# A two-layer decoder trunk: Strassen's seven products in the FFN up projection

## The chip, the cores and the metric

One NeuronCore of one Trainium2 chip runs the whole kernel in one launch. The metric is device time in microseconds (us). Besides the timed runs there is one profiled execution, whose trace gives every row below.

## What is computed

The reference is a trunk of two layers on 512 tokens of width 1024, all in float32. Each layer is a hybrid mixer (attention and mLSTM), a cross-attention into 256 memory tokens and a gated MLP with a short causal convolution. Each of the three is preceded and followed by an RMS norm. Only the MLP matters here:

```python
D_MODEL, SEQ, D_FF = 1024, 512, 2816
def conv_ffn(h, w_up, conv_w, conv_b, w_down):
    u = causal_dwconv(h @ w_up, conv_w, conv_b)      # width 3, per column
    a, g = jnp.split(u, 2, axis=-1)
    return (jax.nn.gelu(g, approximate=True) * a) @ w_down
x = x + rmsnorm(conv_ffn(rmsnorm(x, pre_ffn_g), ...), post_ffn_g)
```

`h @ w_up` is 512 x 1024 by 1024 x 5632, in both layers.

## The kernel before

**Precision.** A product of two float32 operands is made of three matmuls in the faster type fp32r. Each operand is split into a high part (a cast on ACT) and a low part (operand minus high part, on DVE), and `mm3` (L108) adds high by high, high by low and low by high in PSUM. The matmuls are all recorded under L102, the transposes under L106.

**Weights.** `load_unit` (L84) brings in one unit of weights: 128 partitions by 1024 floats, 512 KB, by one DMA from the SP queue into a tile `raw`, of which there are two (`PACE["raw"]`). ACT casts it into `whi` (L89), DVE subtracts into `wlo` (L90), each with five buffers. A `raw` buffer is free for the next load when both have read it. For the up projection a unit is one tile of 128 output columns: eight blocks of 128 by 128, one for each 128 rows of K = 1024. Unit 2j holds tile j of the a half and unit 2j + 1 tile j of the g half; the two together are pair j, of 22.

**The up stage** (`ffn`, L944). The norm in front of it leaves the activations with features on partitions, as four tiles `B` (`xn`): high and low part of each half of K, 128 x 4 x 512. Pairs 0 and 1 run through `feat_halves` (L167), first on tokens 0 to 255, then on 256 to 511, while the norm's last tokens still arrive. The other 20 pairs run through `feat_gen` (L156) unit by unit: 8 blocks x 3 matmuls of 512 columns into one PSUM tile `pg`. When a unit is done, `up_done` (L953) makes the convolution: ACT scales and adds the bias (L958), DVE adds the two delayed terms (L960, two instructions). For the g unit ACT applies the gelu (L965) and DVE multiplies by the a tile (L972) into `gt`. `down` (L986) then multiplies the 22 `gt` tiles by `w_down`.

**Order.** PE's order is that of the program text, with other work slipped in by a count of estimated time (`now`, `tick`). The other engines' order is set by a scheduler. Every engine runs its instructions strictly in that order, and so does the SP queue with its loads: one that waits holds up all behind it.

Of the kernel before, what the change touches and what calls it, by code (L numbers as in the profile page):

```python
# [10 lines left out]
F32 = mybir.dt.float32  # L11
# [9 lines left out]
S = 512  # L21
# [17 lines left out]
def trunk_kernel(ctx: ExitStack, tc: tile.TileContext, x4, memt, w, gw, gains, mcw, fcw, gb,  # L39
# [43 lines left out]

    def load_unit(l, i):  # L84
        raw = pp.tile([128, 1024], F32, tag="raw", name=nm("raw"), bufs=PACE["raw"])
        SP.dma_start(raw, w[l, i])
        hi = pp.tile([128, 1024], F32R, tag="whi", name=nm("whi"), bufs=5)
        lo = pp.tile([128, 1024], F32R, tag="wlo", name=nm("wlo"), bufs=5)
        ACT.copy(hi, raw)  # L89
        DVE.tensor_sub(lo, raw, hi.bitcast(F32))  # L90
        return hi, lo

    def split(src, hi, lo):
# [13 lines left out]

    def mm3(o, lh, ll, rh, rl, start, stop):  # L108
        mm(o, lh, rh, start=start, stop=False)
        mm(o, lh, rl, start=False, stop=False)  # L110
        mm(o, ll, rh, start=False, stop=stop)

# [37 lines left out]
    def drain(tasks, filler=iter(())):  # L150
        while alive(tasks):
            if next(filler, filler) is filler:
                now[0] = max(now[0], min(t[1] for t in side))
            tick()

    def feat_gen(l, u, act, done, n=512):  # L156
        hi, lo = load_unit(l, u)
        acc = pg()
        for k in range(8):
            c = slice(128 * k, 128 * k + 128)  # L160
            rh, rl = act(k)
            mm3(acc[:, :n], hi[:, c], lo[:, c], rh, rl, k == 0, k == 7)
            if k == 7:
                done(acc)
            yield

    def feat_halves(l, units, act, dones, between):  # L167
        ws = [load_unit(l, u) for u in units]
        accs = [pg() for _ in units]
        for half in range(2):  # L170
            if half:
                between()
            cc = slice(256 * half, 256 * half + 256)
            for i, (hi, lo) in enumerate(ws):
                for k in range(8):
                    c = slice(128 * k, 128 * k + 128)
                    rh, rl = act(k)
                    mm3(accs[i][:, cc], hi[:, c], lo[:, c], rh[:, cc], rl[:, cc], k == 0, k == 7)
                    if k % 2:
                        yield  # L180
                if half:
                    dones[i](accs[i])
# [41 lines left out]

    HELD = PACE["held"]

    def pre_norm(t, g, xn, wait):
        xt = xs[t]
# [12 lines left out]
        for h in range(2):  # L241
# [3 lines left out]
            xgs.append(xg)  # L245
        yield wait
        for h in range(2):
            to_feature(xgs[h], t, xn[h], xn[2 + h])
            yield PACE["nh"]

    def to_feature(src, t, hi, lo):
# [6 lines left out]
        DVE.tensor_sub(lo[:, :, c], p3, hi[:, :, c].bitcast(F32))  # L258

    def act_of(xn):  # L260
# [4 lines left out]
    class Tail:  # L265
        def __init__(self, l, gpost, gpre, wait, last=False):
            self.wait = wait
            self.es = ExitStack()
            self.gpost = load_gain(l, gpost)
            self.src = None if last else gpre  # L270
            self.xn = None
            self.hg = {}
            self.v = {}
            self.tasks = []

        def open(self):
            if self.src:
                self.gpre = load_gain(*self.src)
                self.xn = [bt(F32R) for _ in range(4)]
            self.tp = self.es.enter_context(tc.tile_pool(name=nm("tail"), bufs=1, reuse_waits="tile"))  # L280

        def consume(self, h, t, acc):
# [9 lines left out]
            hg = self.tp.tile([128, 512], F32, tag="hg", name=nm("hg"), bufs=6)  # L292
            DVE.tensor_mul(hg, acc, self.gpost[:, c])
# [8 lines left out]
            if self.xn is not None:  # L302
                self.tasks.append(spawn(pre_norm(t, (self.gpre[:, :512], self.gpre[:, 512:]), self.xn, self.wait)))

# [638 lines left out]

    def ffn(l, xn, pend):  # L944
        act = act_of(xn)
# [5 lines left out]
        us = {}  # L951

        def up_done(j, half):  # L953
            m = 22 * half + j

            def f(acc):
                u = fp.tile([128, 512], F32, tag=f"u{half}", name=nm("u"), bufs=2)
                ACT.activation(u, acc, AF.Identity, bias=fcw_t[:, m, 3:4], scale=fcw_t[:, m, 2:3])  # L958
                for q in range(1, 3):
                    DVE.scalar_tensor_tensor(u[:, q:], acc[:, :512 - q], fcw_t[:, m, 2 - q:3 - q], u[:, q:],  # L960
                                             ALU.mult, ALU.add)
                us[half] = u
                if half == 0:
                    return
                ACT.activation(u, u, AF.Gelu_apprx_tanh)  # L965
                if j < 16:
                    if j % 4 == 0:
                        us["big"] = bt()
                    gt = us["big"][:, j % 4, :]
                else:  # L970
                    gt = fp.tile([128, 512], F32, tag="gt", name=nm("gt"), bufs=6)
                DVE.tensor_mul(gt, us[0], u)  # L972
                gtiles.append(gt)
            return f

        first = 0
        if pend:
            first = 4
            drain(pend[:2])
            run(feat_halves(l, [U_UP + i for i in range(4)], act, [up_done(i // 2, i % 2) for i in range(4)],  # L980
                            lambda: drain(pend)))
# [4 lines left out]
    def down(l, fp, gtiles, consume):  # L986
        accs = [[pg() for _ in range(4)], [pa() for _ in range(4)]]
# [7 lines left out]
        for k in range(NF):  # L995
            gh_ = fp.tile([128, 512], F32R, tag="gh", name=nm("gh"), bufs=4)
            gl_ = fp.tile([128, 512], F32R, tag="gl", name=nm("gl"), bufs=4)
            split(gtiles[k], gh_, gl_)
# [18 lines left out]
    for l in range(L):  # L1017
# [12 lines left out]
        es, tasks, o_t = cross(l, xn, pend)  # L1030
        tail = Tail(l, G_POST_MEM, (l, G_PRE_FFN), PACE[f"nffn{l}"])

        def cross_done():
            drain(tasks)
            es.close()
            tail.open()

        run(tok_gen(l, U_WO, act_of([o_t[0], o_t[1], o_t[2], o_t[3]]), (0, 1), tail.consume,
                    seq=early(PACE["ec"], cross_done, lambda u: drain(tasks[u:u + 1]))))
        xn = tail.xn  # L1040
        if l == 0:
            run(fill_k(mem_tiles(pool_mem(tail.tp)), 1, range(PACE["kf"][0])))
        pend = tail.tasks
        tail.close()
        es, fp, gtiles = ffn(l, xn, pend)
        last = l == L - 1
        tail = Tail(l, G_POST_FFN, (l + 1, G_PRE_MIX), PACE["nmix"], last)
        tail.open()
        run(down(l, fp, gtiles, tail.consume))
        xn = tail.xn  # L1050
        pend = tail.tasks
        tail.close()
        es.close()


# [76 lines left out]
```

## Time and profile before

| | |
|---|---|
| time, median of 3 runs | 1598.51 us (1597.74 to 1599.52) |
| time of the profiled execution | 1598.33 us |
| its span in the trace | 1596.5 us |
| PE busy | 1576.7 us (99% of the span) |
| DVE, ACT, POOL busy | 949.1 (59%), 778.8 (49%), 64.6 us (4%) |
| granted TensorE clock | 0.999 of full |

The span is what the trace covers from first to last instruction; the time of the run has 1.8 us around it. A busy share says how long an engine had an instruction in it, not that it was at its peak: matmuls are pipelined, so what one costs is read from the distance between the starts of two, not from its own length. In a row of the timeline, "x2" merges two instructions, and brackets give the idle time before and who ended it.

### The profile page before, as it was taken

To read this page: it belongs to the slowest core of one execution; us is meant where nothing else is said; L and a number is where in the kernel's file an instruction comes from. 1 tells how busy PE (TensorE), PEld (TensorE's weight loads), DVE (VectorE), ACT (ScalarE), POOL (GpSimd) and SP (SyncE) were. 2 spreads that over 40 slices of the span, in tenths; PEclk is the share of its full clock that TensorE was granted. 3 is DMA by queue.
4 is the path that set the end of the run, shared out by engine and by line. 5 is a ranking of instruction groups with operands and counts; after the bars stand their busy time and mean duration, and the time that the engine had idled before them with its cause. 6 is when DMAs were issued, how large, how long until landed. Compare 5 with 4: busy or idle time off the path is not lost.

```text
span 1596.5 us, 21066 instructions
## 1 busy us (share of the span) xinstructions
PE 1576.7 (99%) x8032; PEld 1328.4 (83%) x8032; DVE 949.1 (59%) x1664; ACT 778.8 (49%) x1354; POOL 64.6 (4%) x92
## 2 busy tenths in 40 slices
PE   7999999999999999999999999999999999999998
PEld 5788888998898888888887888889888888888886
DVE  5688555746666555543376876557557655555334
ACT  5677574544554333332356775745445433333222
POOL 0000210100000000000010001101001000000000
PEclk9999999999999999999999999999999999999999
DMA  5322244551253222322323222444512332232221
GB/s 177 124 94 73 95 142 147 160 183 67 67 187 97 102 92 97 101 93 95 103 86 112 93 72 87 144 143 156 171 41 82 106 98 100 93 99 99 93 97 62
DMA packets 55414, 172.91 MB, mean 108 GB/s; under 512 B 6801, under 2 KB 9617, under 8 KB 55314
## 3 DMA queue, kind: packets, MB, share of 16 engines
q1 hardware_dynamic: 55314, 171.57, 32.7%
q8 instruction: 63, 1.03, 0.3%
q14 instruction: 37, 0.30, 0.1%
HBM read 165.22 MB, written 6.33 MB: 107 GB/s over the span
## 4 chain that ended last, share of the span: by engine, by line
PE 87%; DMA 5%; DVE 4%; ACT 3%; issue 1%; POOL 1%; SPq 0%; POOLq 0%; DVEq 0%; ACTq 0%
PE pg L102 69%; PE pa L102 14%; PE pa L106 3%; DMA raw<-in_w_dram 3%; DVE wlo L90 1%; ACT whi L89 1%; DMA raw<-in_memt_dram 1%; DMA raw<-dv 1%; DVE xg L244 1%; DMA raw<-dk 1%; POOL sm L217 0%; ACT junk L222 0%; DVE x L299 0%; DMA dk<-kf 0%; POOL sq L630 0%
## 5 line engine op out<-in xcount | busy, mean ns | idle before, releaser
L102 PE MATMUL pg<-B,whi 128*128 128x512 f32 (+1 forms) x2432 | 693.4, 371 | 2.2 <-DVE ql L925 2.2
L90 DVE TENSOR_TENSOR wlo<-raw,whi 128x1024 fp32r<-128x1024 f32 x268 | 328.8, 1228 | 283.1 <-ACT whi L89 282.7
L102 PEld LDWEIGHTS pg<-B,whi 128*128 128x128 f32 x2432 | 431.6, 189 | 70.0 <-DVE ql L925 2.6
L102 PE MATMUL pg<-B,wlo 128*128 128x512 f32 (+1 forms) x1216 | 447.1, 368 | 0.0
L89 ACT CAST whi<-raw 128x1024 fp32r<-128x1024 f32 x268 | 281.3, 1050 | 293.6 <-PE pg L102 224.7
L102 PE MATMUL pg<-whi,B 128*128 128x512 f32 x896 | 297.5, 398 | 0.0
L102 PEld LDWEIGHTS pg<-B,wlo 128*128 128x128 f32 x1216 | 229.2, 189 | 38.6
L102 PEld LDWEIGHTS pg<-whi,B 128*128 128x128 f32 x896 | 168.5, 188 | 35.1 <-DVE B L95 1.3
L102 PE MATMUL pg<-wlo,B 128*128 128x512 f32 x448 | 175.2, 391 | 0.6 <-DVE sm L236 0.6
L960 DVE SCALAR_TENSOR_TENSOR u<-pg,fcw,u 128x511 f32<-128x511 f32 (+1 forms) x176 | 131.4, 747 | 3.1
L102 PEld LDWEIGHTS pg<-wlo,B 128*128 128x128 f32 x448 | 84.7, 189 | 15.9 <-DVE wlo L90 1.0
L217 POOL TENSOR_TENSOR sm<-sm,mhalf 128x1 f32<-128x1 f32 x56 | 34.3, 612 | 1183.7 <-DVE sm L290 1007.4
L965 ACT ACTIVATE u<-u 128x512 f32<-128x512 f32 x44 | 27.8, 633 | 85.3 <-DVE u L960 85.3
L102 PE MATMUL pa<-whi,gh 128*128 128x512 f32 x176 | 68.6, 390 | 0.0
L102 PE MATMUL pg<-whi,gh 128*128 128x512 f32 x176 | 68.6, 390 | 0.0
L102 PE MATMUL pa<-whi,gl 128*128 128x512 f32 x176 | 68.5, 389 | 0.0
L102 PE MATMUL pa<-wlo,gh 128*128 128x512 f32 x176 | 68.5, 389 | 0.0
L102 PE MATMUL pg<-whi,gl 128*128 128x512 f32 x176 | 68.5, 389 | 0.0
L102 PE MATMUL pg<-wlo,gh 128*128 128x512 f32 x176 | 68.5, 389 | 0.0
L958 ACT ACTIVATE u<-pg,fcw 128x512 f32<-128x512 f32 x88 | 68.1, 774 | 0.0
L95 DVE TENSOR_TENSOR gl<-B,gh 128x512 fp32r<-128x512 f32 x32 | 22.1, 692 | 76.5 <-ACT gh L94 76.4
L94 ACT CAST gh<-B 128x512 fp32r<-128x512 f32 x32 | 19.9, 623 | 92.1 <-PE pg L102 87.0
(215 smaller groups left out, 1956.4 us busy)
## 6 DMA issues: line engine op xcount, KB each, us to landing
raw<-in_w_dram SPq DMA_DIRECT2D x268, 512.0 KB, 3.3
gain<-in_gains_dram SPq DMA_DIRECT2D x11, 512.0 KB, 3.7
raw<-in_memt_dram SPq DMA_DIRECT2D x20, 256.0 KB, 3.0
tb<-tb_d SPq DMA_DIRECT2D x16, 256.0 KB, 4.0
x<-in_x_dram SPq DMA_DIRECT2D x8, 256.0 KB, 5.4
e<-nmu_d SPq DMA_DIRECT2D x8, 256.0 KB, 3.7
dv<-vf SPq DMA_DIRECT2D x8, 256.0 KB, 2.8
dk<-kf SPq DMA_DIRECT2D x16, 128.0 KB, 3.5
```

The lines of the kernel that those rows point to most:

```text
L89: ACT.copy(hi, raw)
L90: DVE.tensor_sub(lo, raw, hi.bitcast(F32))
L94: ACT.copy(hi, src)
L95: DVE.tensor_sub(lo, src, hi.bitcast(F32))
L102: PE.matmul(o, lhs, rhs, **kw)
L106: PE.transpose(o, src, idn)
L217: POOL.tensor_tensor(r, v, mhalf[:, :1], ALU.pow)
L244: DVE.scalar_tensor_tensor(xg, xt[:, c], r, g[h], ALU.mult, ALU.mult)
L958: ACT.activation(u, acc, AF.Identity, bias=fcw_t[:, m, 3:4], scale=fcw_t[:, m, 2:3])
L960: DVE.scalar_tensor_tensor(u[:, q:], acc[:, :512 - q], fcw_t[:, m, 2 - q:3 - q], u[:, q:], ALU.mult, ALU.add)
L965: ACT.activation(u, u, AF.Gelu_apprx_tanh)
```

## The change

Pairs 2 to 21 of each layer are computed by the Strassen-Winograd form. The 2 x 2 blocks are: of the activations, K half by token half (A); of the weights, K half by column tile (B; b11 and b21 are the halves of the a unit, b12 and b22 those of the g unit). Eight products of quarters become seven, each of 4 blocks of K x 3 matmuls of 256 columns: 84 matmuls of 256 columns for a pair in place of 48 of 512.

- **Sums of weights** (`weights`, L1063): POOL makes four sums of 128 x 512 for each pair (L1067 to L1070) into two tiles `T` of 128 x 1024, called t12 and t34 here. ACT and DVE then split four things: the a unit (128 x 1024), t12, t34, and b22 (128 x 512, tile `b`, one buffer). The first three use `whi` and `wlo`, which still have five buffers; `raw` still has two.
- **Sums of activations** (`Forms.add`, L296): `pre_norm` also leaves the activations in float32 (ACT, L275), and when the third and fourth token tiles arrive DVE makes four sums of 128 x 512 for each and splits two of 128 x 1024.
- **Products** (`up_products`, L1053): PE's order for pair j is product 5, 6, then 4 of pair j - 1, 1 of pair j + 1, then 2, 3, 7. The sums of products are made partly by accumulating in PSUM and partly by three copies of 128 x 256 on ACT (L1103, L1121, L1131) and two additions of 128 x 256 on DVE (L1123, L1132). Four matmuls of 512 columns per layer only set PSUM's state.
- **Elsewhere**: the product of gelu and a goes from DVE to POOL (L1041); some of `gt`, the `gh`/`gl` of `down` and the tail's `hg` move into the tiles of `Forms`; `whi` and `wlo` are 1152 wide and used at an offset of 32 floats in the halves and products.

```diff
-    def load_unit(l, i):
+    def load_raw(l, i):
         raw = pp.tile([128, 1024], F32, tag="raw", name=nm("raw"), bufs=PACE["raw"])
         SP.dma_start(raw, w[l, i])
...
+    def w_split(raw, off=0):
+        hi = pp.tile([128, 1152], F32R, tag="whi", name=nm("whi"), bufs=5)[:, off:off + 1024]
+        lo = pp.tile([128, 1152], F32R, tag="wlo", name=nm("wlo"), bufs=5)[:, off:off + 1024]
+        split(raw, hi, lo)
         return hi, lo
...
+        def add(self, t, xf):
+            self.xf[t] = xf
+            if t < 2:
+                return
...
+            DVE.tensor_add(a22, a21, a22)
+            DVE.tensor_sub(a21, a11, a21)
+            DVE.tensor_sub(a11, a22, a11)
+            DVE.tensor_sub(a12, a12, a11)
...
+                split(f, self.s[i][:, :, c], self.s[i + 1][:, :, c])
...
-                DVE.tensor_mul(gt, us[0], u)
+            POOL.tensor_tensor(gt, us.pop((j, 0)), us.pop((j, 1)), ALU.mult)
...
-        for i in range(first, 2 * NF):
-            run(feat_gen(l, U_UP + i, act, up_done(i // 2, i % 2)))
+        run(up_products(l, xn, forms, range(2, NF), up_conv))
...
+        def weights(j):
+            ra, rg = load_raw(l, U_UP + 2 * j), load_raw(l, U_UP + 2 * j + 1)
+            b11, b21, b12, b22 = ra[:, :512], ra[:, 512:], rg[:, :512], rg[:, 512:]
+            t12, t34 = forms.flat(), forms.flat()
+            POOL.tensor_tensor(t12[:, :512], b12, b11, ALU.subtract)
+            POOL.tensor_tensor(t12[:, 512:], b22, t12[:, :512], ALU.subtract)
+            POOL.tensor_tensor(t34[:, :512], b22, b12, ALU.subtract)
+            POOL.tensor_tensor(t34[:, 512:], b21, t12[:, 512:], ALU.subtract)
+            wa = w_split(ra, HALF_OFF)
+            wt = w_split(t12, HALF_OFF)
+            wb = forms.pool.tile([128, 1120], F32R, tag="b", name=nm("b"))
+            wb = wb[:, 96:608], wb[:, 608:1120]
+            split(b22, *wb)
+            wu = w_split(t34, HALF_OFF)
+            return {1: (wa, 0), 2: (wa, 512), 5: (wt, 0), 6: (wt, 512), 3: (wb, 0), 7: (wu, 0), 4: (wu, 512)}
...
+            yield from product(e5, w_, 5, True)
+            p5 = forms.pool.tile([128, 256], F32, tag="p5", name=nm("p5"), bufs=2)
+            ACT.copy(p5, e5)
+            yield from product(e1, w_, 6)
+            DVE.tensor_add(G[:, hv[0]], e1, p5)
+            if j > pairs[0]:
+                yield from last(j - 1)
+            if j < pairs[-1]:
+                yield from first(j + 1)
+            yield from product(A[:, hv[0]], w_, 2)
+            yield from product(G[:, hv[0]], w_, 3)
+            yield from product(e1, w_, 7)
+            ACT.copy(A[:, hv[1]], e1)
+            DVE.tensor_add(G[:, hv[1]], e1, p5)
+            done(j, 1, G)
```

How the built program's order changes is shown at two places. The first is DVE in the middle of the up stage of layer 0. Before, one pair looks like this (`wlo` is a unit's low part, `u` the convolution, the last row the product of gelu and a):

```order
L90 TENSOR_TENSOR wlo_5801<-raw_5798,whi_5800 128x1024
L960 SCALAR_TENSOR_TENSOR u_5649<-pg_5624,fcw_4646,u_5649 128x511
L960 SCALAR_TENSOR_TENSOR u_5649<-pg_5624,fcw_4646,u_5649 128x510
L90 TENSOR_TENSOR wlo_5838<-raw_5835,whi_5837 128x1024
L960 SCALAR_TENSOR_TENSOR u_5684<-pg_5659,fcw_4646,u_5684 128x511
L960 SCALAR_TENSOR_TENSOR u_5684<-pg_5659,fcw_4646,u_5684 128x510
L972 TENSOR_TENSOR B_5689<-u_5649,u_5684 128x512
```

With the change, from t34 of one pair (T_6494; its units are raw_6489 and raw_6491) to b22 of the next (t12 and t34 are T_6620 and T_6621, the units raw_6616 and raw_6618), DVE has:

```order
L100 TENSOR_TENSOR wlo_6511<-T_6494,whi_6510 128x1024
L100 TENSOR_TENSOR wlo_6627<-raw_6616,whi_6626 128x1024
L100 TENSOR_TENSOR b_6507<-raw_6491,b_6507 128x512
L1132 TENSOR_TENSOR pg_4933<-pa_6432,p_1252_6527 128x256
L1024 SCALAR_TENSOR_TENSOR u_6611<-pg_4933,fcw_4652,u_6611 128x511
L1123 TENSOR_TENSOR pg_4935<-pa_6559,p_1268_6654 128x256
L1024 SCALAR_TENSOR_TENSOR u_6611<-pg_4933,fcw_4652,u_6611 128x510
L1024 SCALAR_TENSOR_TENSOR u_6681<-pg_4932,fcw_4652,u_6681 128x511
L1024 SCALAR_TENSOR_TENSOR u_6681<-pg_4932,fcw_4652,u_6681 128x510
L100 TENSOR_TENSOR wlo_6631<-T_6620,whi_6630 128x1024
L100 TENSOR_TENSOR wlo_6638<-T_6621,whi_6637 128x1024
L100 TENSOR_TENSOR b_6634<-raw_6618,b_6634 128x512
```

The split of b22 (the last reader of the g unit's `raw`) stands behind the low parts of t12 and t34 in both pairs; in the first pair it also stands behind the low part of the next pair's a unit (raw_6616), in the second it does not. ACT's casts stand in the same two orders, and the two alternate over the stage.

The second place is POOL. Before, it has nothing in the up stage: its rows pass from the norms before the stage to those after it (each row is one reciprocal root of a norm).

```order
L217 TENSOR_TENSOR sm_4386<-sm_4384,mhalf 128x1
L217 TENSOR_TENSOR sm_4432<-sm_4430,mhalf 128x1
L217 TENSOR_TENSOR sm_4446<-sm_4444,mhalf 128x1
L217 TENSOR_TENSOR sm_7050<-sm_7048,mhalf 128x1
L217 TENSOR_TENSOR sm_7064<-sm_7062,mhalf 128x1
```

With the change it has five instructions for each pair, here from one product of gelu and a to the next:

```order
L1041 TENSOR_TENSOR B_5921<-u_6299,u_6229 128x512
L1067 TENSOR_TENSOR T_6365<-raw_6363,raw_6361 128x512
L1069 TENSOR_TENSOR T_6366<-raw_6363 128x512
L1068 TENSOR_TENSOR T_6365<-raw_6363,T_6365 128x512
L1070 TENSOR_TENSOR T_6366<-raw_6361,T_6365 128x512
L1041 TENSOR_TENSOR B_6430<-u_6426,u_6356 128x512
```

The first of the four sums reads both units (raw_6361 is a, raw_6363 is g), and the fourth is the last of them that reads the a unit.

## Rows read from the trace of the kernel before

**Rows 1.** Windows: start and end of norm, then up stage; engines' busy us, clock, DMA.
```profile
444.00:469.00 25.00, 25.00 (x214) 25.00 (x213) 12.59 (x17) 10.63 (x18) 1.40 (x1) 1.00 0.63 205
480.00:640.00 160.00, 160.00 (x708) 132.48 (x707) 90.27 (x107) 61.19 (x77) 0.00 (x0) 1.00 0.30 99
```
**Rows 2.** Timeline of PE in the up stage: start, length, matmuls of 512 columns.
```profile
565.78 0.61 PE L102 MATMUL pg<-B,whi 128*128 128x512 f32 x2
...
566.46 0.61 PE L102 MATMUL pg<-B,whi 128*128 128x512 f32 x2
```
**Rows 3.** Timeline of PE in the halves of pairs 0 and 1: matmuls of 256 columns.
```profile
474.87 0.40 PE L102 MATMUL pg<-B,whi 128*128 128x256 f32 x2
...
475.23 0.40 PE L102 MATMUL pg<-B,whi 128*128 128x256 f32 x2
```
**Rows 4.** Groups of DVE by line and shape: count, busy us, mean ns of one, idle before.
```profile
L90 DVE TENSOR_TENSOR wlo<-raw,whi 128x1024 fp32r<-128x1024 f32 x268 | 328.8, 1228 | 283.1 <-ACT whi L89 282.7
L960 DVE SCALAR_TENSOR_TENSOR u<-pg,fcw,u 128x510 f32<-128x510 f32 x88 | 65.9, 749 | 3.1
...
L972 DVE TENSOR_TENSOR B<-u,u 128x512 f32<-128x512 f32 x32 | 22.1, 692 | 21.3 <-ACT u L965 21.3
L95 DVE TENSOR_TENSOR gl<-B,gh 128x512 fp32r<-128x512 f32 x32 | 22.1, 692 | 76.5 <-ACT gh L94 76.4
...
L95 DVE TENSOR_TENSOR B<-pg,B 128x256 fp32r<-128x256 f32 x16 | 6.7, 421 | 12.0 <-ACT B L94 12.0
```
**Rows 5.** Groups of ACT by line and shape, the same columns.
```profile
L89 ACT CAST whi<-raw 128x1024 fp32r<-128x1024 f32 x268 | 281.3, 1050 | 293.6 <-PE pg L102 224.7 <-DMA raw<-in_w_dram 61.3 <-issue 3.2
L958 ACT ACTIVATE u<-pg,fcw 128x512 f32<-128x512 f32 x88 | 68.1, 774 | 0.0
...
L965 ACT ACTIVATE u<-u 128x512 f32<-128x512 f32 x44 | 27.8, 633 | 85.3 <-DVE u L960 85.3
...
L94 ACT CAST gh<-B 128x512 fp32r<-128x512 f32 x32 | 19.9, 623 | 92.1 <-PE pg L102 87.0 <-DVE B L972 5.1
...
L94 ACT CAST B<-pg 128x256 fp32r<-128x256 f32 x16 | 6.0, 373 | 19.2 <-PE pg L102 15.4 <-DVE B L95 3.6
```
**Rows 6.** POOL's instructions of L630 and L747: ns min/median/max, first and last start.
```profile
L630 POOL TENSOR_TENSOR sq<-sq,sq x6: 1292/1295/2237, 120.2 to 969.0; 128x512 f32<-128x512 f32 x6
...
L747 POOL TENSOR_TENSOR e<-e,mask x8: 1283/1417/2631, 182.3 to 1030.2; 128x512 f32<-128x512 f32 x8
```
**Rows 7.** Timeline of POOL and DVE around 170 us and around 232 us.
```profile
169.70 2.23 POOL L630 TENSOR_TENSOR sq<-sq,sq 128x512 f32<-128x512 f32 x1 [27.00 <-ACT sq L629]
...
169.58 1.22 DVE L90 TENSOR_TENSOR wlo<-raw,whi 128x1024 fp32r<-128x1024 f32 x1
...
231.42 1.28 POOL L747 TENSOR_TENSOR e<-e,mask 128x512 f32<-128x512 f32 x1 [5.37 <-ACT whi L89]
...
231.72 2.06 DVE L90 TENSOR_TENSOR wlo<-raw,whi 128x1024 fp32r<-128x1024 f32 x1
```
**Rows 8.** Loads of `raw`: landing in the up stage; then DVE, SP, ACT near 322 us.
```profile
DMA to landing us min/median/max: 3.2/3.3/3.4
...
320.77 1.23 DVE L90 TENSOR_TENSOR wlo<-raw,whi 128x1024 fp32r<-128x1024 f32 x1 [1.90 <-ACT whi L89]
...
322.02 0.33 SPq L86 DMA_DIRECT2D raw<-in_w_dram  x1
...
325.80 1.05 ACT L89 CAST whi<-raw 128x1024 fp32r<-128x1024 f32 x1 [1.46 <-DMA raw<-in_w_dram]
```
**Rows 9.** Waits of the SP queue: line, waited for, us in total, times, longest.
```profile
SPq L86 <- DVE wlo L90: 932.8, 201, 12.3
```
**Rows 10.** Timeline of PE at the kernel's start.
```profile
11.54 1.97 PE L106 MATMUL pa<-ident,xg 128*128 128x128 f32 x8 [5.42 <-DVE xg L244]
...
14.52 1.05 PE L102 MATMUL pg<-whi,B 128*128 128x512 f32 x2
15.37 0.46 PE L102 MATMUL pg<-wlo,B 128*128 128x512 f32 x1
```

More of the change, by code (lines that the diff above doesn't have):

```diff
@@ L82, in load_gain, with load_unit @@
         return g
-    def load_unit(l, i):
+    def load_raw(l, i):
         raw = pp.tile([128, 1024], F32, tag="raw", name=nm("raw"), bufs=PACE["raw"])
         SP.dma_start(raw, w[l, i])
[L87 to L90, printed above, removed]
+        return raw
+    def w_split(raw, off=0):
+        hi = pp.tile([128, 1152], F32R, tag="whi", name=nm("whi"), bufs=5)[:, off:off + 1024]
+        lo = pp.tile([128, 1152], F32R, tag="wlo", name=nm("wlo"), bufs=5)[:, off:off + 1024]
+        split(raw, hi, lo)
         return hi, lo
+    def load_unit(l, i, off=0):
+        return w_split(load_raw(l, i), off)
     def split(src, hi, lo):
@@ L154, in drain @@
             tick()
+    HELD = PACE["held"]
+    HALF_OFF = 32
+    PAD_S = 6
     def feat_gen(l, u, act, done, n=512):
@@ L223, in sumsq, with pre_norm @@
         return s_
-    HELD = PACE["held"]
-    def pre_norm(t, g, xn, wait):
+    def pre_norm(t, g, xn, wait, forms=None):
         xt = xs[t]
@@ L246, in pre_norm, with to_feature @@
         yield wait
+        while forms and t == 3 and not forms.s:
+            yield 0.2
+        xf = forms.piece() if forms else None
         for h in range(2):
-            to_feature(xgs[h], t, xn[h], xn[2 + h])
+            to_feature(xgs[h], t, xn[h], xn[2 + h], xf[:, 4 * h:4 * h + 4, :] if forms else None)
             yield PACE["nh"]
-    def to_feature(src, t, hi, lo):
+        if forms:
+            while not forms.free:
+                yield 0.2
+            forms.add(t, xf)
+    def to_feature(src, t, hi, lo, f32=None):
         p = pa()
@@ L265, in trunk_kernel, with __init__ @@
     class Tail:
-        def __init__(self, l, gpost, gpre, wait, last=False):
+        def __init__(self, l, gpost, gpre, wait, last=False, forms=None, room=None):
             self.wait = wait
+            self.forms = forms
+            self.room = room
             self.es = ExitStack()
@@ L951, in ffn @@
         us = {}
-        def up_done(j, half):
[L954 to L971, printed above, removed]
-                DVE.tensor_mul(gt, us[0], u)
-                gtiles.append(gt)
-            return f
@@ L976, in ffn, with up_conv @@
[L976 to L981, printed above, removed]
-        for i in range(first, 2 * NF):
-            run(feat_gen(l, U_UP + i, act, up_done(i // 2, i % 2)))
-        return es, fp, gtiles
-    def down(l, fp, gtiles, consume):
+        def up_conv(j, half, acc):
+            m = 22 * half + j
+            u = fp.tile([128, 512], F32, tag=f"u{half}", name=nm("u"), bufs=2)
+            ACT.activation(u, acc, AF.Identity, bias=fcw_t[:, m, 3:4], scale=fcw_t[:, m, 2:3])
+            for q in range(1, 3):
+                DVE.scalar_tensor_tensor(u[:, q:], acc[:, :512 - q], fcw_t[:, m, 2 - q:3 - q], u[:, q:],
+                                         ALU.mult, ALU.add)
+            if half:
+                ACT.activation(u, u, AF.Gelu_apprx_tanh)
+            us[j, half] = u
+            if (j, 1 - half) not in us:
+                return
+            if j < 16:
+                if j % 4 == 0:
+                    us["big"] = bt()
+                gt = us["big"][:, j % 4, :]
+            elif j < 18:
+                if j == 16:
+                    us["gain"] = pp.tile([128, D], F32, tag="gain", name=nm("gt"), bufs=2)
+                gt = us["gain"][:, 512 * (j - 16):512 * (j - 16) + 512]
+            else:
+                gt = fp.tile([128, 512], F32, tag="gt", name=nm("gt"), bufs=4)
+            POOL.tensor_tensor(gt, us.pop((j, 0)), us.pop((j, 1)), ALU.mult)
+            gtiles.append(gt)
@@ L987, in down @@
+    def down(l, forms, gtiles, consume):
         accs = [[pg() for _ in range(4)], [pa() for _ in range(4)]]
@@ L1041, in trunk_kernel @@
         if l == 0:
-            run(fill_k(mem_tiles(pool_mem(tail.tp)), 1, range(PACE["kf"][0])))
+            run(fill_k(mem_tiles(lambda: tail.forms.wide(F32R)), 1, range(PACE["kf"][0])))
+            tail.forms.free = True
         pend = tail.tasks
         tail.close()
-        es, fp, gtiles = ffn(l, xn, pend)
+        forms = tail.forms
+        es, fp, gtiles = ffn(l, xn, pend, forms)
         last = l == L - 1
-        tail = Tail(l, G_POST_FFN, (l + 1, G_PRE_MIX), PACE["nmix"], last)
+        tail = Tail(l, G_POST_FFN, (l + 1, G_PRE_MIX), PACE["nmix"], last, room=forms.flat)
         tail.open()
-        run(down(l, fp, gtiles, tail.consume))
+        run(down(l, forms, gtiles, tail.consume))
         xn = tail.xn
```

105 lines of the change are left out of this document (93 added, 12 removed).

## Prediction

> **What bounds the kernel now.** I first read the windows of the up stage [rows 1]: in 160 us PE is busy for 160, DVE for 90, ACT for 61 and POOL for none. No engine but PE is near its limit, so a stage costs what its matmuls cost. That cost is the distance between starts. Three matmuls of 512 columns take 566.46 - 565.78 = 0.68 us, 0.227 each [rows 2]; three of 256 take 475.23 - 474.87 = 0.36 us, 0.120 each [rows 3]. A pair now costs 48 x 0.227 = 10.88 us, 20 pairs 217.6 us, twice. Next to be read is how a load of weights is released: the SP queue spends 933 us waiting for a DVE low part, 201 times [rows 9], because there are two `raw` buffers. Today this wait is idle time without a price: a unit's work on ACT and DVE is 1.05 + 1.23 us [rows 4, 5] and a load 3.3 us [rows 8], against 10.88 / 2 = 5.44 us of PE for a unit, with two buffers.
>
> **PE's part.** A pair becomes 84 x 0.120 = 10.08 us, 0.80 less. If nothing else counted, 40 pairs would save 32 us. The four extra matmuls per layer cost 0.9 us.
>
> **The other engines' part, per pair.** DVE: three low parts of 1.228, one of 0.692 (b22), four convolution terms of 0.749, two additions of 0.421 (nearest row, a 128 x 256 subtraction from PSUM) [rows 4]: 8.2 us, before 6.1. ACT: three casts of 1.050, one of 0.623, two of 0.774, a gelu of 0.633, three copies of 0.373 [rows 5]: 7.1 us. POOL: five instructions of 128 x 512 with two inputs; the trace has such ones at 1.29 us when alone [rows 6], so 6.5 us. Each of these fits under 10.08. What decides is in which order they wait for each other.
>
> **POOL and DVE block each other.** At 169.70 a POOL instruction that takes 1.29 us alone took 2.23: DVE had begun a low part at 169.58, which ended at 170.80, and POOL ended 1.13 us after that. At 231.72 DVE began a low part while POOL ran until 232.70; it took 2.06 us and ended 1.08 after POOL [rows 7]. So a POOL sum and a DVE subtraction with both inputs in SBUF run one after the other, the second in 1.13 or 1.08 us from the first's end.
>
> **The loop of releases.** The a unit's `raw` is free when POOL's fourth sum has read it; the g unit's when DVE has made the low part of b22. POOL's first sum needs the g unit. In DVE's and ACT's fixed order b22 stands behind t12 and t34, which come out of POOL's sums of the same pair, and in every second pair also behind the next pair's a unit. So the g load of the next pair cannot start before POOL has finished this pair, and POOL cannot start the next pair before that load has landed. From one g load's issue to the next:
>
> - A pair whose b22 follows t34 directly: load 3.3 [rows 8]; four sums 4 x 1.29 = 5.16 [rows 6]; then low part of t12, blocked until the fourth sum ends, 1.08; POOL's product of gelu and a, which is ready and waits its turn, 1.13; low part of t34, 1.08 [rows 7]; low part of b22, 0.69 [rows 4]. Sum 12.4.
> - A pair whose b22 also follows the next a unit: load 3.3; four sums 5.16; only now is the a unit's buffer free, so the a load, 3.3; its cast 1.05, its low part 1.23, then b22 0.69. Sum 14.7.
>
> Each has some eight hand-overs of 0.02 to 0.03 us (the load at 322.02 was issued 0.02 after the low part that ended at 322.00 [rows 8]): 0.25. Together 27.6 for two pairs, **13.8 us a pair** against 10.88. PE then has 3.7 us of idle time in each pair, and its 0.80 is worth nothing.
>
> How often: pairs 2 to 21 are 20, and the loop holds in the 18 steps from the second's weights to the last's; the first pair's weights are made during the halves and the last has none to make. 18 x (13.8 - 10.88) = 52.6; the other two pairs save 1.6; at the end of the stage the first `gh` and `gl` of the down projection must wait for tiles that product 7 of the last pair reads, and cost a cast and a subtraction in sight, 0.62 + 0.69 [rows 4, 5], before partly hidden; the first wait of the loop in a layer adds about as much. That makes 53 a layer, **106 for both**.
>
> **What lies beside other work.** The float32 copies, activation sums and splits come in the stretch of the norm and the halves: for two token tiles DVE has 2 x (4 x 0.69 + 2 x 1.23) = 10.4 us and ACT some 9, where 25 us have 12.6 and 10.6 busy [rows 1]. They fit in the remaining 12 to 14; without that cover they delay product 5 of the first pair by up to 3 us a layer. I take 0. The copies into PSUM, the additions and the convolution lie between the terms of the loop. The gelu product leaves DVE (0.69) for POOL, where it stands in the loop in every second pair (above). The new places of `gt` and `hg` change no count of instructions. The offset of 32 floats could change the 0.120: in the halves 0.1175 would be 2 us in all; inside the loop nothing.
>
> **Bounds.** The load: 3.2, to the 3.78 us from issue to ACT's start near 322 us [rows 8]. The sum on POOL: 1.13 if one follows another as it followed DVE [rows 7], to 1.42, the median with company [rows 6]. The gelu product: nothing if it is late, to 1.13. All low: 3.2 + 4.52 + 1.08 + 1.08 + 0.69 = 10.6 and 3.2 + 4.52 + 3.2 + 2.97 = 13.9, 12.2 a pair, +47 us. All high: 3.78 + 5.68 + 3.98 + 0.25 = 13.7 and 3.78 + 5.68 + 3.78 + 2.97 + 0.25 = 16.5, 15.1 a pair, +151 us. I take the middle values since they come from this very stage or from undisturbed rows.
>
> A price by page: the Trainium skill, GPSIMD Engine Reference (Elementwise, side-by-side cycle accounting), gives 4497 ns for such an addition of 2048 elements, so by estimate 1.12 us for 512; the trace's 1.29 differs, and by the page the loop would be 0.7 us a pair shorter and the kernel 24 us faster than I say.
>
> **The sum.** The profiled execution took 1598.33 us, as good as the median of 1598.51. 1598.3 + 106 = 1704, and 1705 is the forecast.
>
> **Rivals.**
> - *PE stays the bound (faster).* For it: no engine has more than 8.2 us of work in a pair. Then 1598 - 32 + 2 + about 3 for the stage's ends = 1571. It decides where the loop of releases comes to 20.16 us in two pairs; all but the POOL sums is 27.6 - 10.3 = 17.3, so eight sums would have to take 0.36 us each, against 1.29. It could only come about if the g unit's buffer were free earlier than I read from the order. Chance 0.05.
> - *The shared access is the bound (no change).* If the loop were loose but POOL and DVE excluded each other, a pair would cost 5 x 1.29 + 3 x 1.23 + 0.69 = 10.8 us, 10.88 before: 1598, at most 1600. It needs the same freedom. Chance 0.03.
> - *PE's clock falls in the new gaps (slower still).* After 5.4 us of idle at the start, matmuls of 512 columns stood 0.43 us apart (14.52 to 15.37) instead of 0.227 [rows 10]: the level of 1.2 instead of 2.4 GHz. A pair at the lower level takes 84 x 0.12 x 0.43 / 0.227 = 19 us, and if it held all through, 40 x (19 - 10.9) = +325, 1923. Against it: the gaps are 1 to 3 us each and several in a pair, the work between them is 10 us, and there is slack: product 3, for which the next cast of b22 waits, ends six products (8.6 us) and 1 to 3 us of waiting for copies after t12's low part, and that cast comes 15 us after it by the terms above (14.7 - 9.5 + 8.5 + 1.05). A slower PE for part of the time then costs nothing. A mild form, 15 to 16 us a pair, gives 1750 to 1790. Chance 0.07. The Trainium skill, TensorE: Matmul & The Clock Gate (Part 1), says that the throttled state is the default and that activity releases it, by which idle PE is a risk of its own; these rows agree in the level.
>
> **How the numbers follow.** The forecast has 0.85. Its bounds, 1645 to 1749, with little of the clock's mild form, make the range 1650 to 1755. Differences within 0.2% (3.2 us) can hardly be told from no change in this kernel. Faster 0.05 and the same 0.03 are the first two rivals, slower the rest, 0.92.
>
> **What would show it.** In the changed profile PE busy falls well under 90% in the up stage; the starts of POOL's first sum stand alternately near 12.7 and 15 us apart; a g load is issued right behind each low part of b22, and POOL's first sum starts when it lands; POOL has instructions of up to 2.3 us. The 256-column matmuls stand 0.12 apart. I am wrong if POOL's first sum waits for something else, if PE is busy all through the stage, or if matmuls in it stand 0.22 apart.

## The result, and the profile after

The changed kernel takes 1726.67 us (median of 4 runs, 1721.86 to 1729.15) against 1598.12 us on the same chip: 1.080 times as long, 95% interval 1.0773 to 1.0828. The forecast was 1705 us (1650 to 1755), slower. The profiled execution took 1721.86 us; its span is 1720.1 us, 123.6 us more than before.

Part 1 of the page of the changed kernel, busy us and share of the span:

```profile
PE 1597.7 (93%) x9480; PEld 1404.3 (82%) x9480; DVE 1083.9 (63%) x1804; ACT 895.1 (52%) x1578; POOL 368.5 (21%) x296
```

The up stages hold nearly all of the difference. From pair 2 to the start of the down projection they lasted 217.6 us in either layer; now 274.9 and 280.7. Windows of the two stages, columns as in [rows 1]:

```profile
476.00:751.00 275.00, 225.81 (x1687) 216.67 (x1686) 179.44 (x203) 135.05 (x204) 142.38 (x97) 0.94 0.24 80
1312.00:1593.00 281.00, 229.61 (x1685) 220.30 (x1686) 179.44 (x204) 137.47 (x207) 142.50 (x98) 0.93 0.25 83
```

No engine is full: PE is busy for 82%, DVE for 65, POOL for 52. Before, PE was never idle in the window of [rows 1]. The waits of PE in the first window say for whom it now waits (us in total, times, longest): for casts of sum tiles, for their low parts, and for a copy (L1131) that stands on ACT behind the casts of the next a unit and, in every second pair, of b22.

```profile
PE pa L107 <- ACT whi L99: 18.9, 10, 2.6
PE pg L107 <- ACT pg L1131: 15.5, 12, 1.7
PE pa L107 <- DVE wlo L100: 11.9, 15, 0.9
```

What they wait for in turn is in the chain of waits, here for two pairs (start, length, engine and line; hand-overs and two middle sums left out):

```profile
578.39 1.28 POOL T L1067
...
582.26 1.29 POOL T L1070
...
583.57 3.45 DMA raw<-in_w_dram
...
587.10 1.05 ACT whi L99
...
589.33 0.68 DVE b L100
...
590.04 3.63 DMA raw<-in_w_dram
...
593.80 1.29 POOL T L1067
...
597.63 1.28 POOL T L1070
...
598.93 1.05 ACT whi L99
...
602.15 0.69 DVE b L100
...
602.86 3.47 DMA raw<-in_w_dram
...
606.46 1.29 POOL T L1067
```

This is the forecast's loop of releases, and TensorE is not in it; from 598.66 to 602.23 DVE makes the two low parts, 1.32 and 2.22 us long. The second, which the chain waits for, is the one that is held up, by POOL's product of gelu and a, which runs until 601.14. From first sum to first sum the pair that starts at 578.39 takes 15.41 us: sums, a second load (the next a unit), its cast, b22, the g load. The pair at 593.80 takes 12.66: sums, cast, low parts, b22, the g load. In layer 0 there are 18 such steps: the first 17.60, then nine with a mean of 12.73 and eight with 15.36; their mean is 14.17, layer 1's 14.23 (1316.69 to 1572.78).

SP's waits in the first window say the same from the side of the loads: where all 41 waited for low parts before, now 19 wait for the fourth sum and 20 for the low part of b22 (L1132 is the addition that follows it); 12 more, 24.0 us in all, are for another low part.

```profile
SPq L86 <- POOL T L1070: 141.7, 19, 8.8
SPq L86 <- DVE pg L1132: 53.0, 9, 6.6
SPq L86 <- DVE b L100: 42.2, 11, 7.5
SPq L86 <- DVE wlo L100: 24.0, 12, 5.2
```

Which kind a pair is, the compiled order on DVE decides. From the list of DVE's instructions, two pairs of layer 0 (low parts of sum tiles T, of the next a unit, of b22):

```
641 wlo<-T   642 wlo<-T   643 wlo<-raw (next a)   644 b<-raw
651 wlo<-T   652 wlo<-T   653 b<-raw   654 wlo<-raw (next a)
```

The text of the kernel is the same for every pair; the scheduler chose the order, and turns it round from pair to pair.

### The profile page after: what moved, and what is told of

Its sections match the earlier page's. It is cut to its first block, busy times and chain, and to the rows that moved or that the text cites. A ratio compares the mean times of both kernels' runs of the same rounds, so it can differ in the third digit from the quotient of the medians.

```text
span 1720.1 us, 24569 instructions
## 1 busy us (share of the span) xinstructions
PE 1597.7 (93%) x9480; PEld 1404.3 (82%) x9480; DVE 1083.9 (63%) x1804; ACT 895.1 (52%) x1578; POOL 368.5 (21%) x296
## 4 chain that ended last, share of the span: by engine, by line
PE 49%; DMA 16%; POOL 13%; DVE 9%; issue 7%; ACT 6%; POOLq 0%; SPq 0%; DVEq 0%; ACTq 0%
PE pg L107 33%; DMA raw<-in_w_dram 14%; PE pa L107 13%; ACT whi L99 3%; POOL T L1069 3%; POOL T L1070 3%; POOL T L1067 3%; POOL T L1068 3%; PE pa L111 2%; DVE wlo L100 2%; DVE b L100 1%; DMA raw<-in_memt_dram 1%; POOL sm L226 1%; ACT junk L231 1%; DVE xg L252 1%
## 5 line engine op out<-in xcount | busy, mean ns | idle before, releaser
L107 PE MATMUL pg<-B,whi 128*128 128x256 f32 (+1 forms) x1800 | 425.2, 329 | 36.9 <-ACT pg L1131 30.9
L107 PEld LDWEIGHTS pg<-B,whi 128*128 128x128 f32 x1800 | 293.3, 191 | 61.0 <-ACT pg L1131 35.6
L107 PE MATMUL pg<-B,wlo 128*128 128x256 f32 (+1 forms) x896 | 288.7, 322 | 0.0
L107 PE MATMUL pa<-S,whi 128*128 128x256 f32 x960 | 203.1, 310 | 43.6 <-ACT whi L99 39.5
L100 DVE TENSOR_TENSOR wlo<-T,whi 128x1024 fp32r<-128x1024 f32 x80 | 137.6, 1720 | 122.4 <-ACT whi L99 121.0
L107 PEld LDWEIGHTS pa<-S,whi 128*128 128x128 f32 x960 | 168.4, 215 | 48.8 <-ACT whi L99 44.0
L107 PE MATMUL pa<-S,wlo 128*128 128x256 f32 x480 | 152.1, 317 | 24.3 <-DVE wlo L100 24.2
L1024 DVE SCALAR_TENSOR_TENSOR u<-pg,fcw,u 128x510 f32<-128x510 f32 (+1 forms) x176 | 128.1, 745 | 33.7 <-ACT u L1022 31.2
L107 PE MATMUL pa<-whi,S 128*128 128x512 f32 x352 | 117.5, 393 | 0.0
L107 PE MATMUL pg<-whi,S 128*128 128x512 f32 x352 | 116.1, 390 | 0.8 <-DVE u L1024 0.8
L1067 POOL TENSOR_TENSOR T<-raw,raw 128x512 f32<-128x512 f32 x40 | 53.0, 1325 | 276.7 <-DMA raw<-in_w_dram 188.9
```

The lines of the kernel that those rows point to most:

```text
L100: DVE.tensor_sub(lo, src, hi.bitcast(F32))
L107: PE.matmul(o, lhs, rhs, **kw)
L1067: POOL.tensor_tensor(t12[:, :512], b12, b11, ALU.subtract)
```

## The experiments

Each run was timed beside the kernel before, on the same chip as it (medians of the kernel before: 1596.6 to 1597.3 us).

| run | edit | median us | ratio to before, 95% interval |
|---|---|---|---|
| e1_raw4 | four raw buffers | 1624.85 | 1.0186 [1.0163, 1.0208] |
| e2_b22_first | b22 split early, its tile with two buffers | 1635.54 | 1.0241 [1.0223, 1.0259] |
| e3_double_product5 | product 5 twice | 1789.41 | 1.121 [1.1193, 1.1227] |
| e4_gelu_product_dve | gelu product on DVE | 1672.78 | 1.0477 [1.0462, 1.0493] |
| e5_b22_before_next | order fixed: b22 first | 1682.08 | 1.0527 [1.0512, 1.0541] |
| e6_b22_after_next | order fixed: b22 last | 1844.43 | 1.1554 [1.1533, 1.1575] |
| e7_b22_after_double5 | as e6, product 5 twice | 1840.65 | 1.1523 [1.1507, 1.1539] |
| e8_every_second_pair | seven products in every second pair | 1601.41 | 1.0023 [1.0013, 1.0032] |
| e9_plain_unshifted | as e8, plain pairs at column 0 | 1602.56 | 1.0043 [1.003, 1.0056] |
| e10_three_of_four | in three pairs of four, one order fixed | 1589.77 | 0.9954 [0.9941, 0.9967] |
| e11_no_weight_sums | weight sums left out | 1569.63 | 0.983 [0.9814, 0.9847] |
| e12_raw4_t12_order | as e1, with e10's order | 1632.22 | 1.0211 [1.0194, 1.0228] |

### Opening the loop: e1 and e2

```diff
-            ra, rg = load_raw(l, U_UP + 2 * j), load_raw(l, U_UP + 2 * j + 1)
+            ra = load_raw(l, U_UP + 2 * j)
+            rg = fp.tile([128, 1024], F32, tag="rg", name=nm("rg"), bufs=2)
+            SP.dma_start(rg, w[l, U_UP + 2 * j + 1])
```

> Only in the stage of the seven products, the second raw unit of a pair gets a pair of buffers of its own (four raw buffers there instead of two; the room comes from letting the last four gelu products use buffers that are idle by then). Nothing is computed otherwise. Theory 1, the loop of releases through the raw buffers (load 3.5 us, sums 5.1 us, ACT and DVE work on them, 12.7 and 15.3 us in turn): the next pair's loads no longer wait for this pair's low parts, so the waits of POOL for a load (188.9 us) nearly vanish and the time falls by 80 to 125 us, to 1600 to 1645 us, where the next limit is TensorE's own 10.1 us or the 10.8 us of POOL and DVE together. Theory 2, TensorE at half clock is what costs the time: loads come earlier but the stretches at half clock stay, and the time falls by less than 25 us. Theory 3, POOL's and DVE's blocking of each other is the limit: no change, within 10 us, since the same instructions block each other.

```diff
+            wb = forms.pool.tile([128, 1120], F32R, tag="b", name=nm("b"), bufs=2)
+            wb = wb[:, 96:608], wb[:, 608:1120]
+            split(b22, *wb)
             wt = w_split(t12, HALF_OFF)
-            wb = forms.pool.tile([128, 1120], F32R, tag="b", name=nm("b"))
-            wb = wb[:, 96:608], wb[:, 608:1120]
-            split(b22, *wb)
```

> Two raw buffers as in the changed kernel. The split of quarter b22 is written ahead of the split of the first sum tile instead of behind it, and its tile has two buffers so that it need not wait for product 3 of the pair before. Theory 1, the loop: the second unit's buffer is now released by the last sum that reads it, and both loads of the next pair leave when the four sums are done; the loop becomes 3.7 us of load and hand-over and 5.1 us of sums, 8.9 us, less than TensorE's 10.1, so the time falls by 80 to 120 us, to 1605 to 1645 us. Theory 2, the half clock: under 25 us less. Theory 3, the blocking of POOL and DVE: within 10 us, as no instruction is added or removed.

102 and 91 us less than the changed kernel: both inside theory 1's ranges, far from the 25 and 10 us of the others. More buffers, or an earlier release of the same two, free the same time; so the time lay in the release. (In e2, too, the last four gelu products use buffers that are idle by then.) But e2's steps did not fall to the 8.9 us that I expected: one goes from 562.15 to 573.47, 11.3 us, with 6.4 for the four sums, of which the first is blocked (2.20 us), and 4.3 for the g load, which is issued behind the a load. What still stands above the kernel before, e12 looks at below.

### TensorE's work, and an order that moved with it: e3, e6, e7

```diff
             yield from product(e5, w_, 5, True)
+            yield from product(e5, w_, 5, True)
```

> Product 5 of every pair is computed twice into the same bank, the second run writing over the first: 12 more matmuls a pair, 1.44 us, 57.6 us over both layers, and nothing else. Theory 1, the loop of releases does not pass through TensorE, which waits 49 us in a layer's stage: the time stays within 20 us of the changed kernel's 1727, most of the added work filling waits. Theory 2, the half clock costs the time: the added work fills the pauses behind which the clock falls, so that less of the stage runs at half clock and the time falls by 10 to 40 us. If TensorE's own work is on the path after all: 45 to 60 us longer, 1770 to 1787 us.

It took 63 us more, near the 57.6 of work added: by the numbers, TensorE on the path. The trace says otherwise. The chain by line in e3, 580 to 650 us, holds no PE row:

```profile
by line: DMA raw<-in_w_dram 45.4%; issue 12.9%; POOL T L1070 9.2%; ACT whi L99 7.5%; POOL T L1067 7.3%; POOL T L1068 7.1%; POOL T L1069 7.1%; DVE b L100 4.8%; DVE wlo L100 0.2%; DVE pg L1133 0.2%; ACTq L99 0.1%; POOLq L1067 0.1%
```

and the first sums of its pairs now all stand at the long distance (timeline of POOL):

```profile
606.64 1.28 POOL L1067 TENSOR_TENSOR T<-raw,raw 128x512 f32<-128x512 f32 x1 [5.40 <-DMA raw<-in_w_dram]
622.23 1.29 POOL L1067 TENSOR_TENSOR T<-raw,raw 128x512 f32<-128x512 f32 x1 [5.25 <-DMA raw<-in_w_dram]
```

15.59 here; sixteen steps of the stage have a mean of 15.76. With product 5 twice the scheduler put b22 behind the next a unit in every pair. Of the 63 us, 36 steps x (15.36 - 14.2), or 42, are the order by the changed kernel's own long steps; the long steps grew by 0.40, 14 us, though each holds 1.44 more of TensorE; some 7 us are left open. I had not seen that an edit of TensorE's work reorders DVE. To hold the order fast, e5 to e7:

```diff
+            with ExitStack() as behind:
+                for ins in w_split.ins:
+                    behind.enter_context(tc.issue_after(ins.ins))
+                quarter22()
```

> The opposite order, fixed in every pair: b22 is split behind the next pair's first unit, in the text and on ACT and DVE. Theory 1, the loop: all steps become 15.3 to 15.8 us, and the time rises by 45 to 65 us, to 1770 to 1792 us, though TensorE does no more work; the run with product 5 doubled (1789) would then be explained by its order alone. Theory 2, TensorE's added work made that run long: the order costs under 25 us, below 1752.

> The order of the run before, b22 behind the next unit in every pair, and product 5 of every pair computed twice (57.6 us more for TensorE over both layers). Theory 1, the loop does not pass through TensorE: within 12 us of the run before, the added products lying in TensorE's waits. Theory 2, TensorE's own work is on the path: 45 to 60 us above it.

e6 missed its range (up to 1792) by 52 us, and e7 (the same edit with e3's) equals it within 4 us, as theory 1 said, but not for its reason. The chain of e6 in one step of 17.07 us:

```profile
609.85 1.05 ACT whi L99
...
612.30 4.42 PE pa L106 x22
...
617.09 0.74 DVE u L1023
617.83 1.13 DVE wlo L99
...
618.95 0.61 DVE b L99
```

The edit also puts the next pair's g load and sums behind these two splits in the text, and in the order that came of it the low part of the next a unit, ahead of b22, fell behind a convolution; there the loop does pass through TensorE (4.42 us), and at the lower clock (timeline of PE in e6):

```profile
613.10 0.63 PE L106 MATMUL pa<-S,whi 128*128 128x256 f32 x2
...
613.74 0.63 PE L106 MATMUL pa<-S,whi 128*128 128x256 f32 x2
```

Three matmuls take 0.64 us; from 609 to 616 us the granted clock is 0.76 (0.88 from 500 to 800), and such a stretch comes in nearly every step. At 0.119 us apart the 22 matmuls would take 2.6 us. By estimate, then, up to 1.8 us a step, some 60 us in 36 steps, are the clock: about what the run missed by. e7's steps begin at 15.6 us and go over to 17.3 within the stage, with other chains. The two runs don't tell TensorE's share apart; what they show is that this stage costs 12.7 to 17 us a pair by issue order alone.

### The order alone, and the gelu product: e5 and e4

```diff
+            with ExitStack() as behind:
+                for ins in quarters:
+                    behind.enter_context(tc.issue_after(ins.ins))
+                wa = w_split(ra, HALF_OFF)
...
-            split(b22, *wb)
+            quarters[:] = split(b22, *wb)
```

> Nothing is computed otherwise and no buffer is added; only the issue order is fixed on ACT and DVE: the split of quarter b22 stands ahead of the split of the next pair's first unit in every pair. In the changed kernel the scheduler put it ahead in every second pair (the steps of 12.7 us) and behind in the others (the steps of 15.3 us). Theory 1, the loop of releases: all steps become 12.7 us, some 9 steps a layer lose 2.6 us each, and the time falls by 40 to 50 us, to 1675 to 1690 us. Against the run with the gelu product on DVE (1672.8) it then stands 0 to 15 us higher, and that run gained by its order. Theory 2, TensorE is in the loop: its waits fall due elsewhere and the time stays above 1710.

1682.08, as theory 1 has it. All steps but the first of a layer are of the short kind (timeline of POOL in e5):

```profile
599.32 1.29 POOL L1068 TENSOR_TENSOR T<-raw,raw 128x512 f32<-128x512 f32 x1 [5.30 <-DMA raw<-in_w_dram]
612.03 1.29 POOL L1068 TENSOR_TENSOR T<-raw,raw 128x512 f32<-128x512 f32 x1 [5.33 <-DMA raw<-in_w_dram]
```

So 45 of the 128 us are one choice of order, with the same instructions and buffers.

```diff
-            POOL.tensor_tensor(gt, us.pop((j, 0)), us.pop((j, 1)), ALU.mult)
+            DVE.tensor_mul(gt, us.pop((j, 0)), us.pop((j, 1)))
```

> The product of the gelu and the other half goes back from POOL to DVE, as the kernel before had it; the sums stay on POOL. Theory 1, the loop: the low part of the first sum tile is no longer held up by this product (2.3 us instead of 1.2 in the pairs of 12.7 us), so every second pair is about 1.05 us shorter, 10 us a layer, and the time falls by 12 to 25 us to 1702 to 1715. Theory 2, the half clock: within 8 us. Theory 3, the blocking of POOL and DVE: within 8 us, as the product reads two tiles of SBUF on either engine and blocks as long.

54 us less, more than twice what I expected; again the scheduler had moved b22 ahead in every pair but the first few. Against e5, which has that order too, 9 us are left: steps of 12.32 (610.67 to 622.99) instead of 12.70. Moving the product gives the loop some 0.35 us a pair, not 1.05, since on DVE it stands ahead of b22 as well (0.69 us, at 618.09 in e4).

### TensorE alone: e11

```diff
-            POOL.tensor_tensor(t12[:, :512], b12, b11, ALU.subtract)
...
-            wt = w_split(t12, HALF_OFF)
...
-            wu = w_split(t34, HALF_OFF)
+            wt = w_split(rg, HALF_OFF)
+            wb = tuple(half[:, 512:] for half in wt)
+            wu = wa
```

> Leaves out the four sums of weights on POOL, and the splits of the sum tiles and of b22: the seven products of a pair multiply the split parts of the two raw units in their place, 84 matmuls a pair as before, with the sums of activations, the additions and the convolutions as in the changed kernel. Theory 1, the loop through the sums is all that the change costs: TensorE is the bound, and at the 0.119 us that stand between matmuls of 256 columns in the runs so far a pair takes 9.98 us against 10.88 in the kernel before; 40 pairs save 36 us, less up to 8 us at the start of the stages, so 1561 to 1572 us. Theory 2, seven products of 256 columns cost TensorE something that the distances do not show, its clock above all: above 1580 us.

1569.63 us. TensorE is busy throughout; windows of e11:

```profile
540.00:600.00 60.00, 60.00 (x508) 60.00 (x507) 36.26 (x48) 30.49 (x49) 7.73 (x6) 1.00 0.32 106
```

508 matmuls in 60 us are 0.118 each, 9.92 us a pair. In the middle of the stage that is 0.96 less than before, where 0.80 was forecast; the two stages together last 32 us less (201.0 and 202.1 instead of 217.6 each), the whole kernel 27.6. The seven products are worth what they promise; their sums, and the splits that hang on them, take it away.

### A mixed stage: e8, e9, e10, and what holds e1: e12

These stand on e1's four buffers; e9 and e10 each on the one before.

```diff
+        def plain(j):
+            return j % 2 == 1 or j == 2 * l
...
+            if plain(j):
+                w_ = ws.pop(j)
+                yield from whole(A, w_[0])
...
+                yield from whole(G, w_[1])
```

> Four raw buffers in this stage, as in the first run, and seven products only in every second pair (ten pairs of layer 0, nine of layer 1, whose first such pair starts two later); the pairs between are computed as in the kernel before. POOL and DVE get twice the time for the sums of a pair. Theory 1: with the loop open and the load on DVE and POOL halved, TensorE waits for almost nothing and the saving of 0.80 us a pair comes out: 19 times 0.80 is 15 us, less a few us of waits and of building the sums of the activations, so 1582 to 1593 us, under the kernel before (1597). Theory 3, the blocking of POOL and DVE still holds TensorE up: TensorE waits 10 us a layer or more, and the time is 1597 or more.

1601.41: a miss. Waiting is small (5.1 us in layer 0), but the plain pairs' own matmuls are slower than in the kernel before. Timeline of PE in e8, first and, 23 matmuls on, last row of a unit:

```profile
619.21 0.62 PE L107 MATMUL pg<-B,whi 128*128 128x512 f32 x2
...
624.55 0.39 PE L107 MATMUL pg<-B,wlo 128*128 128x512 f32 x1
```

5.34 / 23 = 0.232 us against 0.227 [rows 2]: in 21 plain pairs of 48 such matmuls 5 us, and with 7.8 us of waits in both stages most of the 15 is gone; about 6 us more, within the two stages, I did not trace.

```diff
-                return [load_unit(l, U_UP + 2 * j + i, HALF_OFF) for i in range(2)]
+                return [load_unit(l, U_UP + 2 * j + i) for i in range(2)]
```

> The run with seven products in every second pair, with one thing changed: the weights of the plain pairs between stand at column 0 of their tiles, as in the kernel before, and not 32 columns in, as the seven products and the first four units have them. In the run with the shift a plain pair's matmuls of 512 columns stood 0.232 us apart (16 k groups of 3 in 11.14 us a pair), against 0.227 in the kernel before. If the shift does that: 0.26 us less in each of 21 plain pairs, 5.5 us, so 1594 to 1598 us. If the sums on POOL beside the matmuls do it: no change, 1600 to 1603 us.

```profile
600.86 0.63 PE L107 MATMUL pg<-B,whi 128*128 128x512 f32 x2
...
606.11 0.40 PE L107 MATMUL pg<-B,wlo 128*128 128x512 f32 x1
```

In e9 the same 23 take 5.25 us, 0.228: the place of the weights does matter, but the 256-column products went from 0.119 to 0.120 at once, TensorE waited some 2 us more a layer, and the time stayed. Why both distances moved is open.

```diff
+            return j % 4 == 2
...
+            with ExitStack() as es:
+                for ins in behind:
+                    es.enter_context(tc.issue_after(ins.ins))
+                wt = w_split(t12, HALF_OFF)
```

> Four raw buffers, plain pairs unshifted and only in every fourth pair (2, 6, 10, 14, 18), seven products in the other 15 of a layer; and the issue order fixed at one place: the split of the first sum tile of a pair stands on ACT and DVE behind the convolution of the pair before, so that no convolution that TensorE's next product waits for stands behind a sum that POOL has not done. Theory 1, with the loop open and the order fixed TensorE is the bound again: 30 pairs save 0.80 to 0.88 us each, 24 to 26 us, less some 8 to 14 us of waits and of the sums of activations that the run with every second pair still showed: 1578 to 1592 us. Theory 3, POOL and DVE hold each other up at three sums in four pairs: TensorE waits 15 us a layer or more, 1597 us or more.

1589.77 us: faster than both kernels, 0.46% under the one before (0.33 to 0.59%). PE's waits in layer 0's stage are down to these (e10, 476 to 700 us):

```profile
PE pg L107 <- DVE u L1026: 2.8, 3, 1.7
PE pg L107 <- ACT pg L1169: 1.5, 3, 0.5
```

> The first run (four raw buffers, all 20 pairs with seven products) with the order of the run with three of four pairs: the first sum tile split behind the convolution of the pair before. Theory 3 as what bounds that first run, POOL's and DVE's blocking of each other (4 sums and a product of 1.2 us on POOL, 3.5 low parts of 1.2 us on DVE, 10.4 to 10.8 us a pair, and the convolutions on DVE as well): the order gives nothing, 1615 to 1635 us. The order as what bounds it: TensorE becomes the bound in all 20 pairs as it did at three of four, and the time falls to 1580 to 1595 us.

1632.22, the number that blocking predicts, and again the number alone would mislead. The chain of e12:

```profile
564.65 1.29 POOL T L1074
...
565.96 0.33 SPq L86
...
566.38 4.23 DMA rg<-in_w_dram
...
570.75 2.27 POOL T L1071
```

and what SP's queue waits for in 520 to 700 us:

```profile
SPq L86 <- POOL T L1074: 88.6, 16, 6.6
```

SP issues the a load of the pair after next ahead of the next pair's g load (in its list raw_5980, then rg_5854, and only after raw_6107 the rg_5982 that belongs to raw_5980); that a load must wait for the fourth sum, and the g load stands behind it. So e1 and e12 still run in a loop of g load (4.2) and four sums, 11.2 us from 559.52 to 570.75, with a wait that the four buffers did not remove but moved into the queue. POOL's blocked sums (2.27 instead of 1.29) lengthen it. An order on SP with the g load first was not tried, so how much of the time the blocking alone would hold is open.

## Why the prediction was right, step by step

**PE's part** (0.120 apart, 0.80 us a pair, no gain from it): the matmuls stand 0.119 apart, and e11, where only this part counts, gives 1569.63; the rival "PE stays the bound" had put that state at 1571. Its condition, sums of 0.36 us or a g buffer that is free earlier, was not met; and e2, which frees that buffer earlier, shows that this alone is not enough (1635.54).

**POOL and DVE block each other**: the product of gelu and a took 2.29 us at 598.85 beside a low part that began at 598.66 and ended at 599.98; the next low part then waited for the product (the two of DVE are one row here).

```profile
598.85 2.29 POOL L1041 TENSOR_TENSOR B<-u,u 128x512 f32<-128x512 f32 x1
...
598.66 3.57 DVE L100 TENSOR_TENSOR wlo<-T,whi 128x1024 fp32r<-128x1024 f32 x2 [4.29 <-ACT whi L99]
```

The Trainium skill, SBUF — State Buffer (SBUF: two separate sides), calls this an exclusive lock held for a whole instruction by a DVE operation with two SBUF inputs or by a GpSimd one; the rows agree.

**The loop of releases, two kinds of pair**: 12.65 and 14.95 us were forecast with hand-overs, 12.73 and 15.36 measured. e1, e2 and e5 break or shorten it and get the time. Its terms: sums 1.25 us from start to start and 1.29 the last, as taken from [rows 6]; the 1.12 that I estimated from the Trainium skill, GPSIMD Engine Reference (Elementwise, side-by-side cycle accounting), did not come. The gelu product, sized at 1.13 in the short kind, holds the low part of t34 up by 1.0 (2.22 us instead of 1.23); e4 against e5 shows only 0.35 because DVE then spends 0.69 on the product itself, ahead of b22.

**What was mis-sized**: 106 us forecast, 123.6 in the trace. The 18 steps take 255.0 and 256.1 us where 18 x 13.8 = 248.4 were forecast, 14.3 us more for both layers. The raw loads take 3.4 to 3.6 us, not 3.3 [rows 8], and the long pair has two of them: with the hand-overs, 0.41 a long step, some 3.3 us a layer. The first step of the loop takes 17.6 and 18.2 us instead of 13.8, because b22's tile of that pair has to wait for product 3 (chain of layer 0: PE until 488.85, cast 0.63, low part 0.70, then the load): another 4 us a layer (in layer 1 I did not follow its chain). In layer 1 the loop also begins later: the sum at 1316.69 starts 4.7 us after the stage's first matmul, in layer 0 the one at 476.24 only 0.3 after it: 4.4 us. There POOL's first sum of the stage had waited 9.33 us, until 1301.89, for a split of the activations' sums, work whose delay the prediction took as 0. And outside the two stages 3.2 us came on, where it took 0 too. These are 21.9; what is left of the stages came out 4.3 lower than taken, although the 53 us a layer leave out the 0.9 us of the four extra matmuls that the prediction itself names.

**The clock**: I gave 0.07 to gaps that slow TensorE and cost time. The gaps did lower it. Timeline of PE after a wait of 2.30 us, then a little later:

```profile
601.06 0.63 PE L107 MATMUL pa<-S,whi 128*128 128x256 f32 x2
...
601.70 0.63 PE L107 MATMUL pa<-S,whi 128*128 128x256 f32 x2
...
606.74 0.40 PE L107 MATMUL pa<-B,whi 128*128 128x256 f32 x2
...
607.09 0.40 PE L107 MATMUL pa<-B,whi 128*128 128x256 f32 x2
```

Three matmuls in 0.64 us, then three in 0.35: 1.2 and 2.4 GHz. Such stretches of 3.4 to 6.8 us come seven times in layer 0's stage, each in a short step. They cost nothing that shows: the short steps, 12.73 with them, are 12.70 in e5, whose windows from 480 to 660 us have the full clock. Time on an engine outside the loop is free, at either level; in e6, where TensorE is in the loop, the same stretches do cost time, by the estimate there.

## What to carry to other kernels

Before trading matmuls for sums, follow the buffer that the sums read from its load to its last reader in each engine's compiled order: an unchanged bound of 10 us of work became 12.7 or 15.4 by whether one small subtraction stood before or behind its neighbour. Where a scheduler sets that order, an edit on one engine can turn it round on another, so an experiment is compared with the order that it got, by the chain, and not by its total alone (e3 came within 3 us of a theory's range, and e12 into one, that their chains don't bear out). Use the dearer scheme only as often as its loads and helper engines, in the order that they have, keep up: with four buffers and one order fixed, three pairs in four won 0.5% (e10) and all of them lost 2.1% (e12); as first built, all of them lost 8%.

## What was unexpected of the hardware

The distance between 512-column fp32r matmuls was 0.227, 0.228 and 0.232 us in three kernels with the same shapes and full clock, and that of 256-column ones 0.119 or 0.120. Between e8 and e9 only the column at which the plain pairs' weights stand moved, and both distances changed; no run shows why. A load of 512 KB took 3.3 us before, 3.4 to 3.6 in the changed kernel's loop and mostly 4.2 in e12, where it is issued 0.4 us behind another.
